# Sixteen gate projections as plain products instead of groups of seven

## The chip, the cores and the metric

The kernel runs on one core of a Trainium2 chip. The metric is the device time of one execution in microseconds; a lower time is better. The core has a matrix engine (TensorE, in the profile PE, with its weight loads as PEld), two elementwise engines (VectorE, DVE, and ScalarE, ACT), GpSimd (POOL) and SyncE (SP), which here only issue transfers for the most part, and 16 DMA engines.

## The reference

One layer of a decoder trunk over 256 positions and 2048 channels. One projection of the normed input h feeds four branches; each is projected to 2048 channels, multiplied by a sigmoid gate that is itself a projection of h, and the four are summed.

```python
h = rmsnorm(x, norm_g)
proj = einsum('bsd,df->bsf', h, w_in)              # 2048 -> 18432
ya = stick_breaking_attention(a_q, a_k, a_v) * silu(a_g)
yb = conformer_conv(b_a, b_b, ...) * silu(b_g)      # 31 taps, LayerNorm over channels
yc = spatial_gating(gelu(c_u), gelu(c_v), ...) * silu(c_g)
yd = dilated_mixture(d_q, d_k, d_v) * silu(d_g)
yproj = einsum('bsnc,ncd->bsnd', stack([ya, yb, yc, yd], 2), w_branch)
gates = sigmoid(einsum('bsd,df->bsf', h, w_gate) + b_gate)   # 2048 -> 4 x 2048
merged = sum(gates * yproj, over n)
out = rmsnorm(x + einsum('bsd,de->bse', merged, w_out), final_g)
```

Everything is float32.

## The kernel before

**Jobs.** The weights lie in HBM as 256 tiles of 128 x 2048 float32, 1 MB each. A *job* is one tile with its matmuls. To keep float32 accuracy, a tile is split into two numbers of a shorter type: ACT rounds it (`hi`, L127), DVE subtracts (`lo`, L134). The moving or stationary side of the product is split in the same way (`xhl` for h, `yh` and `yl` for a branch), and three products stand for one. A projection that leaves channels on the partitions (`proj_t`, `mm_t`, L281 and L284) issues 16 pairs of matmuls of 512 and 256 columns; one that leaves positions there (`mm_n`, L333 to L335) issues 24 matmuls of 512 columns, into two PSUM banks, one for each half of the positions. A gate chunk of 512 channels is four such jobs (`gate_plain`), a branch chunk two (`branch`).

**Order.** The order on PE, ACT, DVE and SP is the order of the program text as `run` (L167) emits it. `prog` is the list of jobs. At step t it issues the loads of jobs up to t + 5, the roundings up to t + 2, the additions up to t + 4 and the subtractions up to t + 2, then the matmuls of job t, its `post`, and what `later` has put down for this step. All four engines work through their queue in that order. POOL, which issues the smaller transfers, is ordered by a planner. Weight tiles have six buffers (`st`), `hi` and `lo` three each; the pool `phase` has two of 128 x 2048, which the branches' `yh` and `yl` share with the masks of the attentions and the constants of the spatial gating.

**Groups.** The gates of the branches b and a, 2 x 2048 channels, are computed in four groups. A group covers two chunks of 512 channels and all 256 positions as a 2 x 2 block product with seven products instead of eight (`group`, L427). Each product has two half jobs of 12 matmuls (`half`, L458). Some use a sum or a difference of weight tiles: `do_load` then loads a second tile, and `do_add` (L122) adds the two on DVE. The matching sums of h are made once by `make_sx` (L382), in four steps, one per job, after the norm of the convolution. The bias enters through one more matmul (L452). Results are combined on DVE (`done`, L441) after copies by ACT (`keep`, L437). The half jobs wait in `queue`; `put` (L160) takes one after every second ordinary job, from the last pair of dilated heads on, and `step(len(queue))` takes the rest ahead of branch a. A half job counts 0.5 in `later`.

**Banks and y.** `n_banks(i)` gives two banks of `ps_n` or `ps_t`; gates always take `n_banks(1)`, branches too, except c. `job_y` (L597) is an empty job ahead of a branch's first one: at `do_add` it loads the branch's y from HBM, and at `do_lo` it splits it into `yh` and `yl`.

**Sequence.** d_v, a_v; b_a and b_b; the dilated heads with the convolution's taps between them on DVE; gates d; b_g; branch d; the stick-breaking heads in pairs (`a_pair`); c_v; branch b; the spatial gating (`c_begin`, `c_norm`, eight `c_unit`); gates c; branch a; branch c; the output projection. The gates' bias of c and d is loaded by `fetch` (tag `ml`, two buffers) and added by DVE (L539); branches use tag `ml` as well, for the running sum that they load from HBM, add to and store (L631, L649, L651).

Of the kernel before, what the change touches and what calls it, by code (L numbers as in the profile page):

```python
# [9 lines left out]
F32 = mybir.dt.float32  # L10
# [15 lines left out]
NEG = -1.0e30  # L26
LOAD_AHEAD = 5
ADD_AHEAD = 4
# [28 lines left out]
def hybrid_block(ctx: ExitStack, tc, w, x, xT, vec, bg, bgb, cst, dmask, sgu_wT, sgu_lg, sgu_lb, sgu_b, final_g, out):  # L57
# [44 lines left out]
    class Job:  # L102
# [3 lines left out]

        def __init__(self, src, mm, plus=None, post=None, keep=None, split=None, prev=None, size=1.0):
            self.src, self.mm, self.plus, self.post, self.keep, self.split = src, mm, plus, post, keep, split
            self.prev, self.size, self.cut = prev, size, False

        def do_load(self):
            src = self.src
            self.st = None if src is None else src() if callable(src) else load(src)
            self.other = load(self.plus) if self.plus is not None else None
            if self.keep is not None:
                self.keep(self.st)

        def do_add(self):
            if self.other is not None:
                if self.prev is not None and not self.prev.cut:  # L120
                    self.prev.do_lo()
                V.tensor_add(self.st[:], self.st[:], self.other[:])  # L122
# [6 lines left out]
        def do_lo(self):  # L129
            if self.split is not None:  # L130
                if not self.cut:
                    self.hl = self.split(self.st)
            elif not self.cut:
                V.tensor_sub(self.hl[1], self.st[:], self.hl[0].bitcast(F32))  # L134
            self.cut = True

    prog, queue, calls = [], [], {}
    now, mains = [0], [0]
# [16 lines left out]
    def step(n=1):  # L155

        for _ in range(min(n, len(queue))):
            prog.append(queue.pop(0))

    def put(job):  # L160

        prog.append(job)
        mains[0] += 1
        if mains[0] % 2 == 0:
            step()

    def run():  # L167
        n = len(prog)
        stages = ((LOAD_AHEAD, "do_load"), (SPLIT_AHEAD, "do_hi"), (ADD_AHEAD, "do_add"), (SPLIT_AHEAD, "do_lo"))
# [207 lines left out]

    sx = {}  # L380

    def make_sx():  # L382

        def pair(name):
            t = st_p.tile([P, 2, KB, P], F32, tag="st", name=name)
            return t[:, 0], t[:, 1]

        def quarter(q, k0, t0):
            V.tensor_add(q, xhl[:, k0:k0 + KB, t0:t0 + P].bitcast(F32), xhl[:, k0:k0 + KB, S + t0:S + t0 + P].bitcast(F32))

        def put(name, src):
            t = s_p.tile([P, 2, KB, P], F32R, tag="s", name=name)
            split(t[:, 0], t[:, 1], src)
            sx[name] = t

        def s1():
            a21, a22 = box["a21"], box["s1"] = pair("a2")
            quarter(a21, 0, P)
            quarter(a22, KB, P)
            V.tensor_sub(a22, a21, a22)  # L400
            put("s1", a22)

        def s2():
            a11, _ = box["a11"], box["a12"] = pair("a1")
            quarter(a11, 0, 0)
            V.tensor_sub(box["s1"], box["s1"], a11)
            put("s2", box["s1"])

        def s3():
            V.tensor_sub(box["a11"], box["a11"], box["a21"])  # L410
            put("s3", box["a11"])

        def n4():
            quarter(box["a12"], KB, 0)
            V.tensor_add(box["a12"], box["a12"], box["s1"])
            put("n4", box["a12"])

        for i, fn in enumerate((s1, s2, s3, n4)):
            later(i + 1, fn)

    def x_part(name):
        if name in ("a11", "a12", "a22"):
            k0, t0 = (0 if name == "a11" else KB), (P if name == "a22" else 0)
            return lambda k, part: xhl[:, k0 + k, part * S + t0:part * S + t0 + P]
        return lambda k, part: sx[name][:, part, k, :]

    def group(expect, sink, bias=None):  # L427


        box, ts, bs = {}, {}, {}  # L430

        def tile_of(c, h, j):
            return expect(c, 2 * h + j)

        def keep(name):
            t = box[name[1]] = so_p.tile([P, 512], F32, tag="so", name=name[1])
            A.activation(t[:], box[name[0]][:], AF.Copy)  # L437

        def done(tb, c, op, a, b, t):
            if op is not None:  # L440
                op(box[t][:], box[a][:], box[b][:])  # L441
            sink(tb, c, box[t], op is not None)

        def half(acc, name, j, src, plus=None, first=False, post=None, keep=None, prev=None):
            def mm(hi, lo):
                lh = x_part(name)
                if first and j == 0:
                    pool, tag = (ps_x, "x") if acc == "X" else (ps_n, "n")
                    ps = box[acc] = pool.tile([P, 512], F32, tag=tag, name=acc)
                    if bias is not None and acc != "Y":  # L450
                        r = bias + (8 if acc == "Z" else 0)
                        T.matmul(ps[:], sel[:, r:r + 1].to_broadcast([P, P]), bgr[:], start=True, stop=False)  # L452
                ps = box[acc]
                fresh = first and j == 0 and (bias is None or acc == "Y")
                for kk in range(4):
                    k, o = 4 * j + kk, kk * 512
                    for i, (part, w_) in enumerate(((0, hi), (0, lo), (1, hi))):
                        T.matmul(ps[:], lh(k, part), w_[:, o:o + 512], start=fresh and kk == i == 0,  # L458
                                 stop=j == 1 and kk == 3 and i == 2, skip_group_check=not first)

            return Job(src, mm, plus=plus, post=post if j else None, keep=keep, prev=prev, size=0.5)

        def held(j):
            return lambda: ts[j]

        V_ = V
        p1 = [half("X", "a11", j, tile_of(0, 0, j), first=True, keep=lambda st, j=j: ts.__setitem__(j, st),
                   post=lambda: keep(("X", "p1"))) for j in range(2)]
        p2 = [half("Y", "a12", j, tile_of(0, 1, j), first=True,
                   post=lambda: done(0, 0, V_.tensor_add, "Y", "p1", "p1")) for j in range(2)]  # L470
        p5 = [half("Z", "s1", j, held(j), plus=tile_of(1, 0, j), first=True, prev=p1[j],
                   post=lambda: keep(("Z", "p5"))) for j in range(2)]
        p6 = [half("X", "s2", j, held(j), plus=tile_of(1, 1, j), prev=p5[j],
                   post=lambda: keep(("X", "u2"))) for j in range(2)]
        p3 = [half("Z", "n4", j, tile_of(1, 1, j),
                   post=lambda: done(0, 1, V_.tensor_sub, "Z", "u2", "u2")) for j in range(2)]
        p7 = [half("X", "s3", j, tile_of(1, 0, j), plus=tile_of(1, 1, j),
                   post=lambda: done(1, 1, V_.tensor_sub, "p5", "X", "p5")) for j in range(2)]
        p4 = [half("X", "a22", j, held(j), plus=tile_of(0, 1, j), prev=p6[j],
                   post=lambda: done(1, 0, None, "X", "X", "X")) for j in range(2)]  # L480
        return p1 + p2 + p5 + p6 + p3 + p7 + p4


# [3 lines left out]

    bgr = cp.tile([P, 512], F32R, name="bgr")
    sel = cp.tile([P, 16], F32R, name="sel")

    def gate_bias_load():
        b0, b1 = box["b0"], box["b1"] = [so_p.tile([P, 512], F32, tag="so", name=f"b{i}") for i in range(2)]
        nc.gpsimd.dma_start(b0[:], bg[0])
        nc.gpsimd.dma_start(b1[:], bg[1])

    def gate_bias():


        b0, b1 = box["b0"], box["b1"]
        V.tensor_add(b0[:], b0[:], b1[:])  # L500
        A.activation(sel[:], cst_sb[:, C_SEL:C_SEL + 16], AF.Copy)
        A.activation(bgr[:], b0[:], AF.Copy)
        V.tensor_sub(bgr[32:64, :], b0[32:64, :], bgr[32:64, :].bitcast(F32))

    def gate_group(b, cc):
        bi = BRANCH[b]

        def sink(tb, c, t, in_sbuf):
            def fn():
                g = t if in_sbuf else so_p.tile([P, 512], F32, tag="so", name="g")  # L510
                A.activation(g[:], t[:], AF.Sigmoid)
                o = (2 * cc + c) * 512
                nc.scalar.dma_start(g_dr[bi, tb, :, o:o + 512], g[:])
                stored.add((b, 2 * cc + c, tb))

            later(1, fn)
# [480 lines left out]
    for i in range(8):  # L997
        c_unit(i)
# [168 lines left out]
```

## Time and profile before

| | us |
|---|---|
| median of three runs | 1589.12 |
| their range | 1582.57 to 1590.14 |
| the profiled execution | 1586.43 |
| its span, first to last instruction | 1583.4 |
| ACT busy (49%) | 776.1 |
| weight loads by SP, 1 MB each | 286 issues, 5.0 to landing (median) |

The mean granted clock of TensorE is 0.976. A matmul's time in the trace is longer than the distance between two starts, because matmuls are pipelined; distances are what counts for throughput. In a row of the trace, the bracket gives the time that the engine was idle just before and the instruction that ended it. In the windows, each engine's busy time in a stretch is followed by its number of instructions.

### The profile page before, as it was taken

To read this page: it belongs to the slowest core of one execution; us is meant where nothing else is said; L and a number is where in the kernel's file an instruction comes from. 1 tells how busy PE (TensorE), PEld (TensorE's weight loads), DVE (VectorE), ACT (ScalarE), POOL (GpSimd) and SP (SyncE) were. 2 spreads that over 40 slices of the span, in tenths; PEclk is the share of its full clock that TensorE was granted. 3 is DMA by queue.
4 is the path that set the end of the run, shared out by engine and by line. 5 is a ranking of instruction groups with operands and counts; after the bars stand their busy time and mean duration, and the time that the engine had idled before them with its cause. 6 is when DMAs were issued, how large, how long until landed. Compare 5 with 4: busy or idle time off the path is not lost.

```text
span 1583.4 us, 18279 instructions
## 1 busy us (share of the span) xinstructions
PE 1487.2 (94%) x7340; PEld 1246.4 (79%) x7340; DVE 1080.6 (68%) x1146; ACT 776.1 (49%) x712; POOL 91.6 (6%) x168
## 2 busy tenths in 40 slices
PE   8999999999998899989999899998799998998997
PEld 6788888888886688777788787877678887876785
DVE  7848888888887776565664665666586765746554
ACT  6444444444444554455446466554266754524442
POOL 0010000000000000001100000011200000021000
PEclk9999999999999899999999999999999999999999
DMA  8675554545452467677864673687875776997551
GB/s 330 214 288 195 185 187 170 193 167 196 162 181 89 169 241 284 246 287 264 283 233 181 251 268 141 234 298 274 314 289 215 267 267 229 365 337 272 187 202 53
DMA packets 62467, 364.60 MB, mean 230 GB/s; under 512 B 8144, under 2 KB 8272, under 8 KB 24880
## 3 DMA queue, kind: packets, MB, share of 16 engines
q1 hardware_dynamic: 43488, 305.29, 52.1%
q0 software_dynamic: 13568, 48.71, 9.2%
q10 hardware_dynamic: 5328, 9.45, 1.6%
q8 instruction: 57, 0.93, 0.2%
q14 instruction: 26, 0.21, 0.0%
HBM read 337.21 MB, written 26.21 MB: 230 GB/s over the span
## 4 chain that ended last, share of the span: by engine, by line
PE 35%; DVE 6%; DMA 6%; ACT 4%; issue 3%; POOL 0%; DVEq 0%; ACTq 0%; POOLq 0%
PE ps L281 6%; DVE lo L134 3%; PE ps L284 3%; PE psy L334 3%; PE X L458 3%; PE psy L333 3%; DMA st<-in_w_dram 3%; PE psy L335 3%; ACT hi L127 2%; PE pso L334 2%; PE pso L335 2%; PE pso L333 2%; PE psg L334 2%; PE psg L333 2%; PE psg L335 2%
## 5 line engine op out<-in xcount | busy, mean ns | idle before, releaser
L134 DVE TENSOR_TENSOR lo<-st,hi 128x2048 fp32r<-128x2048 f32 x272 | 621.2, 2292 | 249.0 <-ACT hi L127 248.9
L281 PE MATMUL ps<-xhl,hi 128*128 128x512 f32 x1920 | 697.5, 406 | 14.9 <-ACT hi L127 5.8
L127 ACT ACTIVATE hi<-st 128x2048 fp32r<-128x2048 f32 x272 | 517.0, 1910 | 249.8 <-PE psy L335 95.3
L284 PE MATMUL ps<-xhl,lo 128*128 128x256 f32 x1920 | 526.9, 285 | 25.9 <-DVE lo L134 25.8
L281 PEld LDWEIGHTS ps<-xhl,hi 128*128 128x128 f32 x1920 | 364.8, 192 | 95.7 <-ACT hi L127 11.4
L284 PEld LDWEIGHTS ps<-xhl,lo 128*128 128x128 f32 x1920 | 369.7, 193 | 41.2 <-DVE lo L134 32.4
L313 ACT ACTIVATE bt<-ps 128x256 f32<-128x256 f32 x120 | 45.8, 382 | 332.1 <-PE ps L281 326.9
L122 DVE TENSOR_TENSOR st<-st 128x2048 f32<-128x2048 f32 x32 | 73.2, 2288 | 76.7 <-DMA st<-in_w_dram 76.7
L333 PE MATMUL psy<-hi,yh 128*128 128x512 f32 x256 | 103.8, 405 | 15.8 <-DVE gl L647 9.3
L689 DVE SCALAR_TENSOR_TENSOR cv<-glu,vec_sb,cv 128x255 f32<-128x255 f32 (+14 forms) x240 | 112.3, 468 | 6.6
L334 PE MATMUL psy<-lo,yh 128*128 128x512 f32 x256 | 103.0, 402 | 5.6 <-DVE lo L134 5.6
L334 PE MATMUL psg<-lo,xhl 128*128 128x512 f32 x256 | 101.1, 395 | 6.1 <-DVE lo L134 6.1
L333 PE MATMUL psg<-hi,xhl 128*128 128x512 f32 x256 | 101.4, 396 | 1.9 <-ACT hi L127 1.9
L335 PE MATMUL psy<-hi,yl 128*128 128x512 f32 x256 | 102.3, 400 | 0.0
L335 PE MATMUL psg<-hi,xhl 128*128 128x512 f32 x256 | 100.9, 394 | 0.0
L314 DVE TENSOR_TENSOR dst<-ps,bt 128x256 f32<-128x256 f32 x120 | 50.6, 421 | 72.9 <-ACT bt L313 72.6
L333 PEld LDWEIGHTS psy<-hi,yh 128*128 128x128 f32 x256 | 49.8, 194 | 30.8 <-ACT hi L127 13.7
L334 PEld LDWEIGHTS psy<-lo,yh 128*128 128x128 f32 x256 | 49.7, 194 | 16.8 <-DVE lo L134 6.8
L334 PEld LDWEIGHTS psg<-lo,xhl 128*128 128x128 f32 x256 | 48.9, 191 | 17.1 <-DVE lo L134 7.0
L333 PEld LDWEIGHTS psg<-hi,xhl 128*128 128x128 f32 x256 | 48.8, 191 | 12.6 <-issue 2.3
L335 PEld LDWEIGHTS psy<-hi,yl 128*128 128x128 f32 x256 | 49.9, 195 | 10.7
L333 PE MATMUL psv<-hi,xuh 128*128 128x512 f32 x128 | 51.6, 403 | 7.0 <-ACT hi L87 7.0
(261 smaller groups left out, 1645.7 us busy)
## 6 DMA issues: line engine op xcount, KB each, us to landing
st<-in_w_dram SPq DMA_DIRECT2D x286, 1024.0 KB, 5.0
gl<-g_dr POOLq DMA_DIRECT2D x32, 256.0 KB, 6.3
m_dr<-gl POOLq DMA_DIRECT2D x24, 256.0 KB, 6.2
ml<-m_dr POOLq DMA_DIRECT2D x24, 256.0 KB, 6.2
g_dr<-g ACTq DMA_DIRECT2D x20, 256.0 KB, 7.0
bgb<-in_bgb_dram POOLq DMA_DIRECT2D x8, 256.0 KB, 7.4
g_dr<-p ACTq DMA_DIRECT2D x8, 256.0 KB, 5.4
xr<-in_x_dram POOLq DMA_DIRECT2D x8, 256.0 KB, 5.0
```

The costliest lines, as they stand in the source:

```text
L122: V.tensor_add(self.st[:], self.st[:], self.other[:])
L127: A.activation(self.hl[0], self.st[:], AF.Copy)
L134: V.tensor_sub(self.hl[1], self.st[:], self.hl[0].bitcast(F32))
L281: T.matmul(ps[:], hi[:, o:o + P], rhs[:, k, :], start=start, stop=stop)
L284: T.matmul(ps[:, 0:S], lo[:, o:o + P], rhs[:, k, 0:S], start=False, stop=False)
L313: A.activation(bt[:], ps[:, S:2 * S], AF.Copy)
L314: V.tensor_add(dst[:, j, :], ps[:, 0:S], bt[:])
L333: T.matmul(ps[tb][:], lh(k0 + kk, 0, tb), hi[:, o:o + 512], start=st, stop=False)
L334: T.matmul(ps[tb][:], lh(k0 + kk, 0, tb), lo[:, o:o + 512], start=False, stop=False)
L335: T.matmul(ps[tb][:], lh(k0 + kk, 1, tb), hi[:, o:o + 512], start=False, stop=sp)
L458: T.matmul(ps[:], lh(k, part), w_[:, o:o + 512], start=fresh and kk == i == 0, stop=j == 1 and kk == 3 and i == 2, skip_group_check=not first)
L689: V.scalar_tensor_tensor(dst, src, wc, dst, op0=ALU.mult, op1=ALU.add)
```

## The change

The groups go, with all that serves them: `make_sx`, `x_part`, `group`, `gate_group`, the bias tiles, `do_add`, the queue of half jobs. All sixteen gate chunks are `gate_plain`, with the bias added by DVE. `put` appends only, so that the order is the written one, and that order is new: gates b stand behind branch d; gates c 0 and c 1, branch b, gates a, branch a, gates c 2 and c 3 follow the spatial gating. Gates and branches take the two pairs of banks in turn, by their chunk. `job_y` is put two jobs ahead of the branch, and loads, rounds and subtracts in the stages of any other job, so that y is split four jobs ahead. Two steps of the convolution's norm are two jobs apart instead of one, and the product with b_g comes two jobs after its hook instead of three.

```diff
+Y_AHEAD = 2
 LOAD_AHEAD = 5
-ADD_AHEAD = 4
+ROUND_AHEAD = 2
...
-            self.other = load(self.plus) if self.plus is not None else None
...
-        def do_add(self):
-            if self.other is not None:
-                if self.prev is not None and not self.prev.cut:
-                    self.prev.do_lo()
-                V.tensor_add(self.st[:], self.st[:], self.other[:])
...
     def put(job):
-
         prog.append(job)
-        mains[0] += 1
-        if mains[0] % 2 == 0:
-            step()
...
-        stages = ((LOAD_AHEAD, "do_load"), (SPLIT_AHEAD, "do_hi"), (ADD_AHEAD, "do_add"), (SPLIT_AHEAD, "do_lo"))
+        stages = ((LOAD_AHEAD, "do_load"), (ROUND_AHEAD, "do_hi"), (SPLIT_AHEAD, "do_lo"))
...
     def gate_plain(b, c):
...
-                    acc["ps"] = n_banks(1, "psg")
+                    acc["ps"] = n_banks(c, "psg")
...
-        def cut(st):
+        def round_y():
             yhl.extend(phase(n, F32R) for n in ("yh", "yl"))
-            split(yhl[0][:], yhl[1][:], box["yf"][:])
-            return ()
-
-        job.do_add, job.split = fetch_y, cut
+            A.activation(yhl[0][:], box["yf"][:], AF.Copy)
+            job.hl = ()
+
+        def rest_y():
+            V.tensor_sub(yhl[1][:], box["yf"][:], yhl[0][:].bitcast(F32))
+
+        job.do_load, job.do_hi, job.do_lo = fetch_y, round_y, rest_y
...
-                    acc[c] = n_banks(c if sink else 1, "psy")
+                    acc[c] = n_banks(c, "psy")
...
-        prog.append(job_y(b, yhl))
+        prog.insert(len(prog) - Y_AHEAD, job_y(b, yhl))
...
-        later(1, lambda: conv_norm_r(csq))
+        later(2, lambda: conv_norm_r(csq))
...
-        later(1, lambda: conv_norm3(red))
+        later(2, lambda: conv_norm3(red))
...
         put_y("b", 0, KB, cv[:])
-        make_sx()
...
-        if h0 == 6:
-            for b in "ba":
-                queue += gate_group(b, 0) + gate_group(b, 1)
...
-            later(3, fn)
+            later(2, fn)
...
     branch("d", first=True)
+
+    for c in range(4):
+        gate_plain("b", c)
...
     v_plain("c_v", AF.Gelu_apprx_tanh)
-    branch("b")
...
     for i in range(8):
         c_unit(i)
+    gate_plain("c", 0)
+    gate_plain("c", 1)
+    branch("b")
     for c in range(4):
-        gate_plain("c", c)
-    step(len(queue))
+        gate_plain("a", c)
     branch("a")
+    gate_plain("c", 2)
+    gate_plain("c", 3)
```

More of the change, by code (lines that the diff above doesn't have):

```diff
@@ L102, in hybrid_block, with __init__ @@
     class Job:
-        def __init__(self, src, mm, plus=None, post=None, keep=None, split=None, prev=None, size=1.0):
-            self.src, self.mm, self.plus, self.post, self.keep, self.split = src, mm, plus, post, keep, split
-            self.prev, self.size, self.cut = prev, size, False
+        def __init__(self, src, mm, post=None, keep=None, split=None, size=1.0):
+            self.src, self.mm, self.post, self.keep, self.split, self.size = src, mm, post, keep, split, size
         def do_load(self):
@@ L130, in do_lo @@
             if self.split is not None:
-                if not self.cut:
-                    self.hl = self.split(self.st)
-            elif not self.cut:
+                self.hl = self.split(self.st)
+            else:
                 V.tensor_sub(self.hl[1], self.st[:], self.hl[0].bitcast(F32))
-            self.cut = True
-    prog, queue, calls = [], [], {}
-    now, mains = [0], [0]
+    prog, calls, now = [], {}, [0]
     def later(n, fn):
@@ L153, in when @@
             later(0.5, lambda: when(ready, fn))
-    def step(n=1):
-        for _ in range(min(n, len(queue))):
-            prog.append(queue.pop(0))
     def put(job):
         prog.append(job)
-        mains[0] += 1
-        if mains[0] % 2 == 0:
-            step()
     def run():
         n = len(prog)
-        stages = ((LOAD_AHEAD, "do_load"), (SPLIT_AHEAD, "do_hi"), (ADD_AHEAD, "do_add"), (SPLIT_AHEAD, "do_lo"))
+        stages = ((LOAD_AHEAD, "do_load"), (ROUND_AHEAD, "do_hi"), (SPLIT_AHEAD, "do_lo"))
         begun = [0] * len(stages)
@@ L374, in first_job @@
         return Job(src, mm, split=cut)
[L380 to L481, printed above, removed]
@@ L486, in hybrid_block @@
     m_dr = dr_p.tile([2, P, D], F32, name="m_dr")
[L488 to L516, printed above, removed]
-        return group(lambda c, q: ("gateN", bi * 4 + 2 * cc + c, q), sink, bias=bi * 2 + cc)
     def gate_plain(b, c):
@@ L671, in hybrid_block @@
           6: lambda: h_split(1), 7: lambda: h_split(2), 8: lambda: h_split(3), 9: h_rstd,
-          10: lambda: d_out(0), 11: lambda: d_out(1), 12: lambda: a_out(0), 13: gate_bias_load,
-          15: lambda: later(1, lambda: (a_out(1), gate_bias()))}
+          10: lambda: d_out(0), 11: lambda: d_out(1), 12: lambda: a_out(0), 15: lambda: later(1, lambda: a_out(1))}
     for i, fn in at.items():
```

## The prediction

> **What bounds the kernel now.** The page first, its busy shares.
>
> ```profile
> span 1583.4 us, 18279 instructions
> PE 1487.2 (94%) x7340; PEld 1246.4 (79%) x7340; DVE 1080.6 (68%) x1146; ACT 776.1 (49%) x712; POOL 91.6 (6%) x168
> ```
>
> PE is the engine that sets the time, so the question is where it loses any. The windows by stage say it: PE busy time is the second number, PEclk the granted clock.
>
> ```profile
> core 0: us, PE busy (x) PEld busy (x) DVE busy (x) ACT busy (x) POOL busy (x), PEclk, DMA share, GB/s
> 120.00:480.00 360.00, 359.91 (x2063) 314.02 (x2062) 301.51 (x512) 163.84 (x178) 3.86 (x6) 1.00 0.51 181
> 480.00:560.00 80.00, 64.54 (x324) 53.91 (x323) 57.13 (x70) 35.90 (x40) 0.54 (x1) 0.89 0.36 133
> 560.00:690.00 130.00, 123.41 (x551) 101.97 (x550) 83.68 (x59) 60.58 (x46) 3.42 (x6) 0.99 0.72 262
> 740.00:800.00 60.00, 55.94 (x231) 45.40 (x231) 35.87 (x24) 25.56 (x17) 7.89 (x15) 0.94 0.75 269
> 800.00:1000.00 200.00, 187.59 (x996) 159.49 (x995) 122.88 (x93) 114.62 (x107) 5.13 (x9) 0.97 0.60 221
> 1060.00:1165.00 105.00, 86.60 (x376) 70.90 (x376) 67.52 (x57) 44.08 (x32) 16.10 (x28) 0.92 0.78 283
> 1290.00:1380.00 90.00, 84.46 (x357) 68.93 (x356) 55.37 (x31) 42.46 (x29) 3.21 (x6) 0.96 0.77 286
> 1380.00:1485.00 105.00, 93.97 (x403) 74.21 (x403) 63.55 (x55) 34.32 (x23) 20.33 (x38) 0.97 0.80 295
> ```
>
> Read the first row against the others. From 120 to 480 only plain projection jobs run, with the convolution and most of the dilated attention beside them on DVE (84% busy), and PE never stops. The products of the groups begin later, by the first start in their row of the tile view:
>
> ```profile
> L458 PE MATMUL X<-hi,xhl x128: 387/389/476, 518.3 to 1378.2; 128*128 128x512 f32 x128
> ```
>
> In the seven rows below the first, PE stands still for 15.5 + 6.6 + 4.1 + 12.4 + 18.4 + 5.5 + 11.0 = **73.5 us**. After a longer stall it also runs at half rate: one minus PEclk times the length gives 8.8 + 1.3 + 3.6 + 6.0 + 8.4 + 3.6 + 3.2 = 35 us. That counts idle time inside a slow stretch twice, as this 5 us window shows, where 2.5 us are charged while PE works 0.84:
>
> ```profile
> 525.00:530.00 5.00, 0.84 (x2) 0.34 (x2) 2.40 (x2) 2.84 (x4) 0.00 (x0) 0.50 0.00 0
> ```
>
> Weighing the slow windows by the work in them I get about 25 us (bounds 15 and 35). So about **98 us** of PE time are lost in these rows.
>
> Who makes PE wait? One such place in the timeline, DVE's rows and then PE's:
>
> ```profile
> 675.43 2.29 DVE L122 TENSOR_TENSOR st<-st 128x2048 f32<-128x2048 f32 x1 [7.53 <-DMA st<-in_w_dram]
> 677.64 2.28 DVE L134 TENSOR_TENSOR lo<-st,hi 128x2048 fp32r<-128x2048 f32 x1
> 679.84 1.28 DVE L539 TENSOR_TENSOR g<-psg,bgb 128x512 f32<-128x512 f32 x2
> ```
>
> ```profile
> 680.67 0.47 PE L281 MATMUL ps<-xhl,hi 128*128 128x512 f32 x1 [4.05 <-DVE g L539]
> ```
>
> The addition of two weight tiles (L122), which only the groups need, stood in DVE's queue for 7.5 us until its second tile had landed. The split and the gate's eviction stood behind it, and PE stood behind them. Over the run L122 has 76.7 us of such waits (its row is below). A product lasts half as long as a job, yet asks for a full split and often for two loads.
>
> **The change part by part.** *More PE work.* A matmul of 512 columns costs this much at full clock:
>
> ```profile
> 1119.15 0.39 PE L334 MATMUL psy<-lo,yh 128*128 128x512 f32 x1
> ...
> 1120.96 0.39 PE L458 MATMUL X<-hi,s 128*128 128x512 f32 x1
> ```
>
> Eight starts in 1.81 us: 0.226 us each. A group is 7 products of 24 matmuls and two for the bias, 170; four groups are 680. The same gates as plain products are 4 x 8 jobs x 24 = 768. **+88 matmuls, +19.9 us**, all on the bounding engine.
>
> *Less work elsewhere.* The rows:
>
> ```profile
> L134 DVE TENSOR_TENSOR lo<-st,hi 128x2048 fp32r<-128x2048 f32 x272 | 621.2, 2292 | 249.0 <-ACT hi L127 248.9
> L127 ACT ACTIVATE hi<-st 128x2048 fp32r<-128x2048 f32 x272 | 517.0, 1910 | 249.8 <-PE psy L335 95.3
> L122 DVE TENSOR_TENSOR st<-st 128x2048 f32<-128x2048 f32 x32 | 73.2, 2288 | 76.7 <-DMA st<-in_w_dram 76.7
> L539 DVE TENSOR_TENSOR g<-psg,bgb 128x512 f32<-128x512 f32 x16 | 10.6, 687 | 1.6 <-PE psg L335 1.6
> ```
>
> 56 half jobs become 32 jobs: 24 splits go (DVE 24 x 2.29 = 55 us, ACT 24 x 1.91 = 46 us), the 32 additions go (73 us), and 32 repeated loads of 1 MB. New are 32 additions of the bias at 0.69 us (22 us); 12 additions of products of about the same length and 12 copies on ACT go. So DVE loses over 110 us and ACT over 45 us. Neither ends last, so by itself none of this is credited. What it buys is that the stalls go, and I price those stage by stage.
>
> *480 to 560.* Two stalls:
>
> ```profile
> 502.15 0.79 PE L281 MATMUL ps<-xhl,hi 128*128 128x512 f32 x1 [5.07 <-DVE dst L314]
> ...
> 527.63 0.80 PE L281 MATMUL ps<-xhl,hi 128*128 128x512 f32 x1 [5.44 <-ACT hi L127]
> ```
>
> The first is the convolution's norm: its reciprocal root, a product of 2.3 us and eight SiLU on ACT stand ahead of a split. That code stays. With two jobs instead of one between its steps, the reduction over channels no longer stands directly ahead of it, and I leave it 4.5 us and 2.9 of slow clock. The second lies in make_sx (four sums of x, each with a split, one per job), which goes. This row falls from 15.5 + 6 to about 7.5.
>
> *560 to 690 and 740 to 800.* The additions go, and the gates alternate between two pairs of banks, so the next chunk needs no eviction. One handover stays behind the gates of d and one behind those of b: the first projection takes the bank of the last chunk's first half and waits for one L539, 0.7 us, with its latency 0.9. Branch d waited for a late y split and for its own eviction (4.1 us in its row); y is now rounded four jobs ahead and the banks alternate: nothing left.
>
> *800 to 1000.* One pair of attention heads puts Abs, Exp and Ln with two table loads ahead of a split; ACT's first row is the end of a projection, DVE's the split that came late, PE's the price.
>
> ```profile
> 854.71 0.38 ACT L313 ACTIVATE bt<-ps 128x256 f32<-128x256 f32 x1 [3.25 <-PE ps L281]
> ```
>
> ```profile
> 863.04 2.29 DVE L134 TENSOR_TENSOR lo<-st,hi 128x2048 fp32r<-128x2048 f32 x1 [7.03 <-ACT hi L127]
> ```
>
> ```profile
> 865.39 0.39 PE L284 MATMUL ps<-xhl,lo 128*128 128x256 f32 x1 [1.54 <-DVE lo L134]
> ```
>
> The chain began at 854.7, and the split was ready at 865.3, 10.6 us later. Two full jobs of 5.6 us (360 us / 2063 x 32 in the clean row) with the score products cover 11.9; a half job in between does not. I leave 1 us a pair, 4 in all (bounds 0 and 12.4).
>
> *1060 to 1165.* Here the groups' additions and second loads met branch b and the gating norm; the last row is the landing time of a branch's load:
>
> ```profile
> 1108.18 0.77 PE L333 MATMUL psy<-hi,yh 128*128 128x512 f32 x1 [5.02 <-DVE gl L647]
> ...
> 1149.43 0.45 PE L284 MATMUL ps<-xhl,lo 128*128 128x256 f32 x1 [4.42 <-DVE lo L134]
> ```
>
> ```profile
> ml<-m_dr POOLq DMA_DIRECT2D x24, 256.0 KB, 6.2
> ```
>
> After the change v is stored just ahead of the norm instead of eight jobs before. Two evictions of 0.7 us, a store and a load of 6.2 us each end some 14 us after v's last product; the norm's place on DVE comes 11.2 us after it. DVE would wait 3 us, with two jobs of split in hand: 1 us for PE (bounds 0 and 5). v keeps one pair of banks: 0.9 us twice.
>
> *1290 to 1485.* Branch c needed its y in the two buffers that branch a still held, and its transposes cost a little:
>
> ```profile
> ACT yh L87 <- PE psy L334: 15.2, 1, 15.2
> ```
>
> ```profile
> 1471.69 0.50 PE L333 MATMUL psy<-hi,yh 128*128 128x512 f32 x1 [1.88 <-DVE ml L1020]
> ```
>
> Eight gate jobs now lie between branch a and branch c, so the wait of 15.2 us goes. The transposes stay: 1.9 us shown, and I allow nearly as much for the other three, 3.3 in all.
>
> *Order and queues.* POOL's place for each load is the planner's. Tag ml has two buffers, for the bias and for a branch's running sum, and a gate's bias is now asked for while branch b or a still runs:
>
> ```profile
> L649 DVE TENSOR_TENSOR gl<-gl,ml 128x512 f32<-128x512 f32 x24 | 16.6, 692 | 1.4 <-DMA ml<-m_dr 0.6
> ```
>
> At best it comes after the sum and costs nothing. At worst it holds one of the two buffers, so in two chunks of two branches the second load begins only after the first addition: 4 x 7 us of DVE waiting, with at most the same on PE. I take 2, because these additions have waited only 0.6 us in all for ml so far. SP issues fewer loads, at 190 GB/s plus 70 for a branch, below the 283 to 295 of the rows above.
>
> **Sum.** Left over: 7.5 + handovers 3.6 (four) + 4 + 1 + 3.3 + 2 = 21 us of 98. Saved 77, paid 19.9: span 1583.4 - 57 = 1526. The profiled execution took 1586.43, 3.0 more than its span, which makes **1529**; the median of the three runs shown, 1589.12, is 2.7 above that execution, inside their spread of 7.6. I forecast 1530.
>
> The clock deserves a look of its own:
>
> ```profile
> 804.79 0.55 PE L284 MATMUL ps<-xhl,lo 128*128 128x256 f32 x1 [1.97 <-DVE lo L134]
> 805.00:810.00 5.00, 5.00 (x21) 4.29 (x22) 4.14 (x2) 0.00 (x0) 0.00 (x0) 0.67 0.97 369
> ```
>
> A stall of 2 us was already followed by half rate, 1.65 us lost. The Trainium skill ("TensorE: Matmul & The Clock Gate", "What's actually happening") says that the clock falls after at least one idle window of about 3.4 us; the row does not agree, and the row decides. By the rule only the stalls above that length (5.07, 5.44, 4.05, 5.02 and 4.42 among the rows shown) would carry clock losses, by my estimate 15 us instead of 25, and the sum would be 1539.
>
> **The rivals.** *A: half of the stalls come back.* The stages keep their own burdens (a norm, a softmax with table loads, 0.75 MB of extra traffic per chunk and pair), and the y splits, the norm with its late v and the ml buffers cost more than I gave them. For it: the 5.07 us stall has nothing to do with the groups. Against it: 120 to 480, with as dense side work, lost nothing. Half of 98 saved: 1586.4 + 19.9 - 49 = 1557; a third saved: 1574.
>
> *B: slower.* The stalls belong to the stages, and the half jobs only happened to be what PE waited at. Then taking them out returns less than the 19.9 us it costs, and from savings below 20 us on the change loses; with none saved 1606. For it: 12.4 us at the attention pairs, where the releaser is L134 behind Exp and Ln. Against it: the 76.7 us that DVE stood before L122 cannot outlive L122. The Trainium skill ("Perfetto Trace Analysis", "Optimization Strategy") says that regimes bound by different engines may gain by being interleaved, which speaks for the old order; the rows so far show the interleaved stretches as the ones that stall, so the trace does not agree.
>
> **How the numbers follow.** Forecast 0.70 (1510 with almost nothing left over, to 1548 with 20 us more than I allowed or the smaller clock term); A 0.22, mostly between 1548 and 1574; B 0.08. The likeliest is 1530. The range 1510 to 1568 leaves out B, the end of A and a little below. What a measurement of this kernel can tell from no change is 0.5%, 8 us: faster takes the forecast and nearly all of A, 0.90; within 0.5% is the end of A and the start of B, 0.03; slower 0.07.
>
> **What would show it.** The profile after should have about 88 more matmuls, no L122, some 24 fewer splits, PE windows as full as 120 to 480 from 560 on, and one stall of 4 to 6 us at the convolution's norm. Wrong would be: repeated PE stalls in the branches with loads of ml or gl as the last releaser (A), waits at the splits in the attention pairs as long as now (B), or DMA shares near 1 while PE waits.

## The result and the profile after

| | before | after |
|---|---|---|
| median of four executions | 1586.69 us | 1509.70 us |
| ratio (95% interval) | | 0.951 [0.9473, 0.9546] |
| profiled execution | 1586.43 us | 1509.23 us |
| its span | 1583.4 us | 1507.3 us |
| mean granted clock | 0.976 | 0.995 |

One of the four executions after was disturbed (3805.53 us); it is left out of the ratio, and the other three lie between 1506.80 and 1510.16.

The forecast was 1530, with a range of 1510 to 1568. The sign came as predicted, and so, in the main, did the mechanism, but the gain is 77 us where the prediction's sum had 57: the time lies 0.3 us below the range. Those 0.3 us are less than the spread of the executions; the 20 us to the forecast are not.

The page of the changed kernel, its busy shares, the chain that ended last, and the lines of the subtraction and of PE's first matmul:

```profile
span 1507.3 us, 18226 instructions
PE 1476.0 (98%) x7428; PEld 1248.4 (83%) x7428; DVE 946.2 (63%) x1080; ACT 704.2 (47%) x657; POOL 94.8 (6%) x174
...
PE 88%; DVE 5%; DMA 3%; ACT 2%; issue 1%; POOL 0%; DVEq 0%; ACTq 0%
...
L125 DVE TENSOR_TENSOR lo<-st,hi 128x2048 fp32r<-128x2048 f32 x248 | 566.9, 2289 | 375.9 <-ACT hi L119 366.0
L261 PE MATMUL ps<-xhl,hi 128*128 128x512 f32 x1920 | 682.4, 401 | 4.7 <-DVE dst L294 4.3
```

PE has the 88 more matmuls (7428 against 7340) and yet is busy for 11.2 us less; its idle time fell from 1583.4 - 1487.2 = 96.2 to 1507.3 - 1476.0 = 31.3. Idle -64.9 and busy -11.2 are the 76.1 by which the span shrank. The subtraction runs 24 times less (248 against 272), as predicted.

The windows of the changed kernel, cut at its own stages (columns as before):

```profile
480.00:540.00 60.00, 55.62 (x304) 48.13 (x304) 39.45 (x57) 28.18 (x34) 0.54 (x1) 0.94 0.49 177
540.00:690.00 150.00, 149.80 (x722) 125.65 (x722) 80.11 (x65) 67.86 (x60) 12.05 (x22) 1.00 0.69 245
690.00:800.00 110.00, 110.00 (x487) 91.09 (x486) 54.07 (x32) 43.53 (x28) 7.03 (x13) 1.00 0.70 240
800.00:1000.00 200.00, 199.52 (x1082) 171.98 (x1081) 100.04 (x86) 109.42 (x107) 9.78 (x16) 1.00 0.54 194
1000.00:1120.00 120.00, 120.00 (x662) 103.80 (x662) 77.03 (x83) 79.29 (x77) 11.95 (x21) 1.00 0.68 243
1120.00:1320.00 200.00, 199.22 (x879) 164.67 (x878) 110.52 (x78) 78.64 (x48) 29.62 (x55) 1.00 0.82 282
1320.00:1410.00 90.00, 86.10 (x380) 69.90 (x379) 56.44 (x44) 35.06 (x26) 10.19 (x19) 0.98 0.76 263
```

From 540 to 1320 PE stands still for 1.5 us in 780, at full clock. Before, these stages held the attention pairs, branch b and the gates, and lost in every row that the prediction shows. What is left behind the start is one stall at the convolution's norm, the transposes of the merged sum in branch c (L862, L866), and two short waits for a split; the waits of PE show them (us in total, times, longest):

```profile
PE psv L313 <- ACT hi L88: 7.6, 2, 6.4
PE ps L261 <- DVE dst L294: 4.3, 1, 4.3
PE psv L314 <- DVE lo L125: 2.7, 4, 1.1
PE psy L313 <- DVE ml L866: 1.9, 1, 1.9
PE pt L862 <- DVE gl L491: 1.3, 2, 0.7
PE psg L314 <- DVE lo L125: 1.2, 2, 0.8
...
PE ps L261 <- DVE g L380: 0.4, 2, 0.2
PE cc L748 <- DVE pr_a L739: 0.3, 1, 0.3
```

The first and the third row belong to the first 80 us of the kernel, as before. Gone is what was the largest row of this view of the kernel before:

```profile
PE ps L284 <- DVE lo L134: 25.8, 14, 5.3
```

### The profile page after: what moved, and what is told of

It is laid out like the page before. It is cut to its first block, busy times and chain, and to the rows that moved or that the text cites. A ratio compares the mean times of both kernels' runs of the same rounds, so it can differ in the third digit from the quotient of the medians.

```text
span 1507.3 us, 18226 instructions
## 1 busy us (share of the span) xinstructions
PE 1476.0 (98%) x7428; PEld 1248.4 (83%) x7428; DVE 946.2 (63%) x1080; ACT 704.2 (47%) x657; POOL 94.8 (6%) x174
## 4 chain that ended last, share of the span: by engine, by line
PE 88%; DVE 5%; DMA 3%; ACT 2%; issue 1%; POOL 0%; DVEq 0%; ACTq 0%
PE ps L261 29%; PE ps L264 14%; PE psg L314 7%; PE psg L315 7%; PE psg L313 7%; PE psy L313 3%; PE psy L315 3%; PE psy L314 3%; DMA ml<-m_dr 2%; PE psv L314 2%; PE psv L315 2%; PE pso L314 2%; PE pso L315 2%; PE pso L313 2%; PE psv L313 2%; DVE lo L125 2%
## 5 line engine op out<-in xcount | busy, mean ns | idle before, releaser
L125 DVE TENSOR_TENSOR lo<-st,hi 128x2048 fp32r<-128x2048 f32 x248 | 566.9, 2289 | 375.9 <-ACT hi L119 366.0
L261 PE MATMUL ps<-xhl,hi 128*128 128x512 f32 x1920 | 682.4, 401 | 4.7 <-DVE dst L294 4.3
L119 ACT ACTIVATE hi<-st 128x2048 fp32r<-128x2048 f32 x248 | 473.5, 1911 | 323.3 <-PE psg L315 181.4
L264 PE MATMUL ps<-xhl,lo 128*128 128x256 f32 x1920 | 519.5, 281 | 0.0
L261 PEld LDWEIGHTS ps<-xhl,hi 128*128 128x128 f32 x1920 | 357.3, 189 | 83.0 <-DVE dst L294 4.6
L264 PEld LDWEIGHTS ps<-xhl,lo 128*128 128x128 f32 x1920 | 363.5, 189 | 9.3
L314 PE MATMUL psg<-lo,xhl 128*128 128x512 f32 x512 | 199.4, 390 | 1.2 <-DVE lo L125 1.2
L313 PE MATMUL psg<-hi,xhl 128*128 128x512 f32 x512 | 199.8, 390 | 0.0
L315 PE MATMUL psg<-hi,xhl 128*128 128x512 f32 x512 | 199.2, 389 | 0.0
L314 PEld LDWEIGHTS psg<-lo,xhl 128*128 128x128 f32 x512 | 96.1, 188 | 21.9 <-DVE lo L125 2.1
L315 PEld LDWEIGHTS psg<-hi,xhl 128*128 128x128 f32 x512 | 96.1, 188 | 20.1
L313 PEld LDWEIGHTS psg<-hi,xhl 128*128 128x128 f32 x512 | 96.1, 188 | 19.6
L314 PE MATMUL psy<-lo,yh 128*128 128x512 f32 x256 | 100.3, 392 | 0.0
L314 PEld LDWEIGHTS psy<-lo,yh 128*128 128x128 f32 x256 | 48.5, 189 | 10.1
```

The source lines that it names most:

```text
L119: A.activation(self.hl[0], self.st[:], AF.Copy)
L261: T.matmul(ps[:], hi[:, o:o + P], rhs[:, k, :], start=start, stop=stop)
L264: T.matmul(ps[:, 0:S], lo[:, o:o + P], rhs[:, k, 0:S], start=False, stop=False)
L313: T.matmul(ps[tb][:], lh(k0 + kk, 0, tb), hi[:, o:o + 512], start=st, stop=False)
L314: T.matmul(ps[tb][:], lh(k0 + kk, 0, tb), lo[:, o:o + 512], start=False, stop=False)
L315: T.matmul(ps[tb][:], lh(k0 + kk, 1, tb), hi[:, o:o + 512], start=False, stop=sp)
```

## The experiments

Two theories, numbered so in the expectations. *Theory 1, the queue:* what PE lost came from waits in DVE's queue (the addition for its second tile, above all), from one pair of banks and from y split late; the change takes these waits away. *Theory 2, the work:* half jobs and additions simply ask more of DVE and ACT than half a job of PE covers, so only less work helps. The runs named b_ and g_ start from the kernel before, those named a_ from the changed one. Ratios are to the kernel before, run beside each on the same chip.

| run | median us | ratio (95%) | span, us | clock |
|---|---|---|---|---|
| b_no_second_load | 1551.32 | 0.9784 [0.9761, 0.9808] | 1552.4 | 0.981 |
| b_no_add | 1546.24 | 0.9749 [0.9726, 0.9771] | 1543.9 | 0.982 |
| b_add3 | 1544.61 | 0.9740 [0.9717, 0.9763] | 1541.1 | 0.983 |
| g_plain_only | 1534.50 | 0.9676 [0.9650, 0.9701] | 1532.2 | 0.991 |
| g_tuned | 1537.20 | 0.9689 [0.9668, 0.9710] | 1537.5 | 0.986 |
| a_banks1 | 1526.76 | 0.9639 [0.9622, 0.9656] | 1523.9 | 0.994 |
| a_make_sx | 1521.01 | 0.9583 [0.9562, 0.9604] | 1520.3 | 0.991 |
| a_branches_adjacent | 1517.51 | 0.9579 [0.9563, 0.9595] | 1516.1 | 0.991 |
| a_conv1 | 1513.37 | 0.9554 [0.9538, 0.9570] | 1512.5 | 0.993 |
| a_y0 | 1511.26 | 0.9543 [0.9527, 0.9560] | 1511.6 | 0.994 |
| a_same | 1510.47 | 0.9517 [0.9497, 0.9537] | 1505.2 | 0.995 |
| a_same2 | 1510.43 | 0.9529 [0.9504, 0.9555] | 1505.3 | 0.997 |
| a_norm_split | 1509.55 | 0.9508 [0.9482, 0.9534] | 1507.8 | 0.995 |
| a_ml3 | 1507.43 | 0.9506 [0.9484, 0.9528] | 1506.2 | 0.995 |
| a_ml3_norm | 1503.51 | 0.9479 [0.9458, 0.9501] | 1503.0 | 0.995 |

### What the additions cost

b_no_second_load: the addition adds the first tile to itself.

```diff
-            self.other = load(self.plus) if self.plus is not None else None
+            self.other = self.st if self.plus is not None else None
...
```

> The kernel before, but the 32 second tiles are not loaded: the addition adds the first tile to itself, so three of seven products in each group and a fourth take other weights. DVE's work and the half jobs stay. Theory 1 (the additions stood in DVE's queue until the second tile had landed): most of the 76.7 us before L122 and most of PE's stalls go, time 1520 to 1545. Theory 2 (a half job asks for a whole split of 2.3 us DVE and 1.9 us ACT in 2.7 us of PE, whatever is loaded): no more than 15 us go, 1570 or above.

b_no_add: neither the second load nor the addition.

```diff
-            self.other = load(self.plus) if self.plus is not None else None
+            self.other = None
...
```

> The kernel before without the second loads and without the additions, so some products take other weights; 56 half jobs stay. Theory 1: within 8 us of the run without second loads. Theory 2: at least 20 us below that run, since 73 us of DVE work leave; what then still stands between it and the changed kernel, less 19.9 us of PE work, is due to half jobs, banks, y and order.

b_add3: everything is computed, but the additions are issued three jobs ahead (and with them the load of a branch's y, which is issued at the same step).

```diff
-ADD_AHEAD = 4
+ADD_AHEAD = 3
```

> The kernel before with the additions issued three jobs ahead instead of four, one job further behind their loads; everything is computed. Theory 1: the wait before L122 falls from 76.7 to below 45 us and the time by 15 to 40 us, 1550 to 1572. Theory 2: within 8 us of before.

The additions in the groups by line of b_no_second_load, then of b_add3; the last field is DVE's idle time ahead of them, 76.7 us in the kernel before:

```profile
L124 DVE TENSOR_TENSOR st<-st 128x2048 f32<-128x2048 f32 x32 | 73.1, 2285 | 23.1 <-DMA st<-in_w_dram 23.1
```

```profile
L122 DVE TENSOR_TENSOR st<-st 128x2048 f32<-128x2048 f32 x32 | 73.1, 2285 | 10.1 <-DMA st<-in_w_dram 10.1
```

The first run fell between the theories' ranges, 35 us below the kernel before: without a second tile the addition still stood 23.1 us in the queue, for the job's own first tile. The second lies 5 us below the first, inside the 8 us of theory 1. The third one settles it, and by more than theory 1 had expected (1550 to 1572). It keeps every load and every addition, and is as fast as the second, which has neither (1544.61 and 1546.24, intervals that overlap). So, once the additions no longer wait long, their 73 us and the 32 MB of second loads cost nothing that these runs can tell; what cost 42 us, more than half of what the change brings, is that an addition issued four jobs ahead came to the head of DVE's queue before its tiles had landed, with the next subtraction behind it. Theory 2 falls for the additions.

### What the groups cost beyond that

g_plain_only: only the groups go; banks, y, order of the branches and the norm stay as before.

```diff
-        make_sx()
...
-        if h0 == 6:
-            for b in "ba":
-                queue += gate_group(b, 0) + gate_group(b, 1)
...
-            later(3, fn)
+            later(2, fn)
...
     branch("d", first=True)
+    for c in range(4):
+        gate_plain("b", c)
...
-    step(len(queue))
+    for c in range(4):
+        gate_plain("a", c)
```

> The groups alone undone: gates b behind branch d and gates a ahead of branch a as plain products, but one pair of banks, y split two jobs ahead, branch b behind c_v, branches a and c next to each other, and the convolution's norm as before (the product with b_g two jobs after its hook, as in the changed kernel). If the groups made the stalls: 1530 to 1545, with the wait of y for branch a's buffers (about 9 us of PE) and the handovers left. If the stages' own burdens made them (rival A or B): 1557 or above.

The waits of PE in this run:

```profile
PE ps L281 <- DVE dst L314: 5.1, 1, 5.1
PE psy L333 <- DVE gl L647: 4.7, 15, 1.4
PE psy L333 <- ACT hi L127: 3.6, 1, 3.6
...
PE psg L333 <- DVE g L539: 2.2, 11, 0.2
PE psy L334 <- DVE lo L134: 1.9, 1, 1.9
```

1534.50, inside the expectation: with 88 more matmuls it is 52 us below the kernel before. The waits for a split are nearly gone, and in their place stand 26 short ones for evictions (L647, L539), from the single pair of banks. The rows of 3.6 and 1.9 us are the wait of y for branch a's buffers.

g_tuned goes the other way: the groups stay, with the additions three jobs ahead, y split early, the norm's steps two jobs apart, the product with b_g two jobs after its hook and the branches in an order near the new one.

```diff
-ADD_AHEAD = 4
+ADD_AHEAD = 3
+Y_AHEAD = 2
...
-        prog.append(job_y(b, yhl))
+        prog.insert(len(prog) - Y_AHEAD, job_y(b, yhl))
...
-        later(1, lambda: conv_norm3(red))
+        later(2, lambda: conv_norm3(red))
...
-    for c in range(4):
-        gate_plain("c", c)
+    gate_plain("c", 0)
+    gate_plain("c", 1)
+    branch("b")
+    gate_plain("c", 2)
     step(len(queue))
     branch("a")
+    gate_plain("c", 3)
```

> The groups kept, with what else was found: additions three jobs ahead, y split early, branch b behind gates c 0 and 1, one gate chunk between branches a and c, the norm's steps two jobs apart; one pair of banks, as the groups need the other. It has 19.9 us of matmuls less than the changed kernel. If the half jobs themselves still crowd DVE and ACT: 1522 to 1536, slower than the changed kernel. If only the waits for second tiles did harm: 1510 or below.

Its largest waits of PE:

```profile
PE ps L285 <- DVE lo L135: 16.0, 13, 2.0
PE X L459 <- DVE p L442: 8.7, 1, 8.7
```

It stays at 0.9689 (1537.20, just above the 1522 to 1536 expected), against 0.9639 for a_banks1 below, which has plain products with the same early y, the same norm, a similar order and also one pair of banks. So even with their worst wait mended, the groups cost some 8 us (0.005 of 1586) more than the 19.9 us of matmuls that they save. What they still pay for are the half job that has to be split in half a job's time (13 waits, none over 2.0 us), the results that must be combined before a bank comes free (one wait of 8.7 us), and make_sx, which alone costs 10.5 us in the run below; no run takes these three apart inside the groups. Here theory 2 has a part. The Trainium skill ("Perfetto Trace Analysis", "Optimization Strategy") says that interleaving may help a kernel whose most-contended engine changes over time. That condition is not met here, for PE is the busiest engine with the half jobs and without, so g_tuned against a_banks1, 0.005 slower, is no test of the sentence.

### Undoing one part of the change

a_banks1, one pair of banks again:

```diff
-                    acc["ps"] = n_banks(c, "psg")
+                    acc["ps"] = n_banks(1, "psg")
...
-                    acc[c] = n_banks(c, "psy")
+                    acc[c] = n_banks(c if sink else 1, "psy")
```

> The changed kernel with one pair of banks for every gate chunk and for the branches b, a and d, as before. In the run with the groups alone undone, a gate chunk lasted 22.25 us where 96 matmuls take 21.75, and a branch chunk 11.35 to 11.93 where 48 take 10.87. By that 15 handovers of gates at 0.5 us and 11 of branches at 0.5 to 1.1 cost 13 to 20 us: 1523 to 1530. If the banks are hidden anyway: within 4 us of 1509.7.

Two neighbouring matmuls of its timeline (start, length, ..., idle time before), the second one the first on a bank that had to be emptied:

```profile
541.87 0.40 PE L315 MATMUL psg<-hi,xhl 128*128 128x512 f32 x1
542.50 0.51 PE L313 MATMUL psg<-hi,xhl 128*128 128x512 f32 x1 [0.23 <-DVE dst L294]
```

1526.76 lies inside the expectation. The span is 16.6 us longer than after the change. The trace shows only 7.5 us more idle time in PE's timeline (28.7 against 21.2); the other 9.1 us are counted as PE busy (1485.1 against 1476.0). The two rows tell where part of them is: the starts are 0.63 us apart instead of 0.227, so the stop costs 0.40, but only 0.23 of it is shown as idle. The rest, 0.17, is the overlap of two matmuls (0.40 long, 0.227 apart) that has to be built up anew; it counts as PE busy. Taken over all stops whose two rows are both single matmuls, start to start less the idle shown and less 0.227 us (0.117 behind 256 columns), this is 7.2 us in 43 stops here, 2.2 in 12 after the change, and 7.9 in 41 before it. That places 5.0 of the 9.1 us; where the other 4 lie, this count does not show. The Trainium skill ("Perfetto Trace Analysis", "Matmuls") says that independent groups of matmuls should rotate through different banks, so that evacuation overlaps with the next group; this run agrees, with some 17 us.

a_make_sx, the four sums of x put back alone:

```diff
         put_y("b", 0, KB, cv[:])
+        make_sx()
```

> The changed kernel with make_sx put back alone, its sums unused: four steps of 3.6 to 5 us on DVE and 1.1 us on ACT, one per job, behind the convolution's norm. If these steps made the second stall before (5.4 and 1.5 us with slow clock behind): 8 to 13 us above the run of the changed kernel. If it was the half jobs that began there: within 3 us of it.

PE's stops in its timeline behind the norm:

```profile
513.63 0.80 PE L261 MATMUL ps<-xhl,hi 128*128 128x512 f32 x1 [4.28 <-DVE dst L294]
523.64 0.49 PE L610 MATMUL s<-dst 128*128 128x128 f32 x2 [1.53 <-DVE dst L294]
529.39 0.45 PE L635 MATMUL pp<-cst_sb,ph_d 128*128 128x128 f32 x1 [4.82 <-DVE ph_d L629]
530.57 0.45 PE L636 MATMUL pp<-cst_sb,ph_d 128*128 128x128 f32 x1 [0.74 <-DVE ph_d L629]
```

10.5 us over a_same, as expected, and at the place expected: the last three stops are new, together 7.1 us, with a slow clock behind them. Not all of it lies there: a short wait for a split behind branch b (L314, 0.8 us after the change) was 2.1 us in this run.

a_branches_adjacent (the last two gates of c ahead of branch a, so that branches a and c share the y buffers again), a_conv1 (the norm's steps one job apart) and a_y0 (no y ahead):

```diff
-        prog.insert(len(prog) - Y_AHEAD, job_y(b, yhl))
+        prog.insert(len(prog) - (0 if sink else Y_AHEAD), job_y(b, yhl))
...
-    branch("a")
     gate_plain("c", 2)
     gate_plain("c", 3)
+    branch("a")
```

> The changed kernel with gates c 2 and c 3 ahead of branch a, so that branch c follows branch a directly and its y has to wait for the two buffers of branch a's y (its split two jobs ahead, since four would never get the buffers). Before, that place cost 3.6 and 2.0 us of idle time and some slow clock: 6 to 10 us more, 1516 to 1520.

```diff
-        later(2, lambda: conv_norm_r(csq))
+        later(1, lambda: conv_norm_r(csq))
...
-        later(2, lambda: conv_norm3(red))
+        later(1, lambda: conv_norm3(red))
```

> The changed kernel with the steps of the convolution's norm one job apart, as before. In the run with the groups alone undone this place cost 1.4 and 5.1 us of idle time against 4.3 in the changed kernel: 2 to 4 us more, 1511 to 1514.

```diff
-Y_AHEAD = 2
+Y_AHEAD = 0
```

> The changed kernel with y split two jobs ahead of its branch instead of four. Before, branch d lost 2.8 us of idle time to the late split, branch b 1.8 us. If that comes back at all four branches, with slow clock behind some: 5 to 15 us more, 1515 to 1525. If the emptier queues of ACT and DVE take the split in two jobs as well: within 4 us of 1509.7.

The first costs about 7 us; its waits of PE show two new rows, at the first matmuls of a branch:

```profile
PE psy L313 <- ACT hi L119: 3.6, 1, 3.6
...
PE psy L314 <- DVE lo L125: 1.9, 1, 1.9
```

The second costs about 3 us and the third 1, by medians against the 1510.4 of the unchanged runs. By the ratios to the kernel before, the three cost 8 to 10, 4 to 6 and 2 to 4 us. Only the interval of the first parts from those of both unchanged runs; a_conv1 overlaps with a_same2, and a_y0 with both, so these two parts stay undecided. a_y0 shows no wait of PE for a late y split at all, which speaks for the second case of its expectation.

### What the changed kernel still loses

a_same and a_same2 are the changed kernel itself, run on the same chip as a_norm_split and as a_ml3.

> The changed kernel itself, beside the others of this call on the same chip: 1505 to 1511. It is what the three below are read against, and what the four runs that undid one part are read against as a ratio to the kernel before.

> The changed kernel again, beside the two below on the same chip: 1505 to 1511.

a_norm_split spreads the norm's product and its eight SiLU over three jobs, so that a split can pass between them:

```diff
-        V.tensor_mul(cv[:], cv[:], bc8(rs[:]))
-        for i in range(8):
-            A.activation(cv[:, i, :], cv[:, i, :], AF.Silu, ...)
-        put_y("b", 0, KB, cv[:])
+        def part(i0, n):
+            V.tensor_mul(cv[:, i0:i0 + n, :], cv[:, i0:i0 + n, :], rs[:].unsqueeze(1).to_broadcast([P, n, S]))
+            for i in range(i0, i0 + n):
+                A.activation(cv[:, i, :], cv[:, i, :], AF.Silu, ...)
+            put_y("b", i0, n, cv[:, i0:i0 + n, :])
+
+        for h in range(3):
+            later(h + 1, lambda h=h: part((0, 3, 6)[h], (3, 3, 2)[h]))
```

> The changed kernel with the last step of the convolution's norm spread: root as now, then product and SiLU for 3, 3 and 2 of the eight channel groups in the next three jobs. If the one stall left in the middle (4.3 us idle, with 3 us of slow clock) is ACT's and DVE's queue behind that step, it goes: 4 to 8 us less than the changed kernel, 1500 to 1506. If not: no change, within 2 us.

A miss: the time is that of a_same. The stall at the norm did go, but PE then met another one, here in its timeline, with the windows around it:

```profile
1191.75 0.50 PE L314 MATMUL psg<-lo,xhl 128*128 128x512 f32 x1 [2.91 <-DVE lo L125]
```

```profile
1190.00:1195.00 5.00, 3.25 (x10) 2.60 (x11) 5.00 (x3) 0.57 (x1) 0.87 (x2) 0.78 0.63 182
1195.00:1200.00 5.00, 5.00 (x21) 4.04 (x20) 1.10 (x1) 1.06 (x1) 0.00 (x0) 0.87 0.94 354
```

The same place in the changed kernel, DVE's timeline:

```profile
1182.59 0.69 DVE L493 TENSOR_TENSOR gl<-gl,ml 128x512 f32<-128x512 f32 x1 [1.75 <-DMA ml<-m_dr]
1183.20 0.69 DVE L491 TENSOR_TENSOR gl<-psy,gl 128x512 f32<-128x512 f32 x1
1189.19 0.69 DVE L493 TENSOR_TENSOR gl<-gl,ml 128x512 f32<-128x512 f32 x1 [5.31 <-DMA ml<-m_dr]
1189.80 6.69 DVE L125 TENSOR_TENSOR lo<-st,hi 128x2048 fp32r<-128x2048 f32 x3
```

DVE stands 5.31 us for a running sum in tag ml, whose load waited for one of two buffers (the runs below test this), and three subtractions stand behind it. In the changed kernel PE's price here is 0.78 us; where PE reaches this place earlier, it is 2.91 us and a slower clock. Hence a third buffer, alone (a_ml3) and with the split norm (a_ml3_norm):

```diff
-    sm2_p = ctx.enter_context(tc.tile_pool(name="ml", bufs=2))
+    sm2_p = ctx.enter_context(tc.tile_pool(name="ml", bufs=3))
```

> The changed kernel with three buffers instead of two for tag ml. In the changed kernel DVE waits 22.6 us for loads of ml, because a gate's bias holds one of the two buffers while branch b or a runs, and a split that stood behind such a wait held PE up for 0.8 us. If that is so: the waits fall below 3 us, the time by 0 to 2 us. If DVE waits for another reason (DMA bandwidth): 22 us of waits as now.

> Three buffers for ml and the norm's last step spread. The spread alone started the gates 4.4 us earlier against the sum ahead of it, but lost 2.9 us of idle time and some slow clock again behind a wait for ml in the branch. If both readings hold: 4 to 7 us below the changed kernel of this call. If the stalls only move: within 2 us of it.

DVE's waits for ml, 22.8 us in a_same2, are out of the list of a_ml3 and 3.2 us in a_ml3_norm, so it was the buffer that the loads waited for; PE's waits for a split there (L314, 1.2 us after the change) are gone in both. Alone, neither edit can be told from the changed kernel beside it (intervals overlap); together they give 1503.51, some 7 us less, as expected, with intervals that just part (0.9501 and 0.9504). It is the fastest version here, 5.2% below the kernel before.

## Why the prediction came out as it did

**Right.** PE stayed the bound. The added matmuls cost what they should: their number is 88, and in the gates of the changed kernel 23 starts take 5.22 us, 0.227 us each:

```profile
584.67 0.39 PE L313 MATMUL psg<-hi,xhl 128*128 128x512 f32 x1
...
589.89 0.39 PE L315 MATMUL psg<-hi,xhl 128*128 128x512 f32 x1
```

L122's wait was the largest single cause (42 us, b_add3). make_sx's stall went, for 10.5 us. The norm's stall stayed, predicted at 4 to 6 us:

```profile
512.41 0.80 PE L261 MATMUL ps<-xhl,hi 128*128 128x512 f32 x1 [4.28 <-DVE dst L294]
```

The transposes were given 3.3 us and took 1.3 + 1.9. The trouble with two ml buffers came as described (22.6 us of DVE waiting in six places), and cost PE 1.2 us of idle time instead of 2.

**Right for another reason, or wrong without weight.** Branches start without a wait for y, as predicted, but the earlier split is not shown to be the reason: in a_y0, without it, PE does not wait for y either. The prediction counted 32 new additions of the bias; 16 are new (L539 ran 16 times before, L380 runs 32 times after). Neither enters the sum. DVE's busy time fell by 134.4 us and ACT's by 71.9.

**Rivals.** A and B both asked for PE stalls that stay in the stages from 540 on; the windows from 540 to 1320 hold 1.5 us. B's ground, that plain jobs would stall at the same places, fell with g_plain_only already: its window 800 to 1000, 12.4 us of idle time before, is as full as that of the changed kernel.

```profile
800.00:1000.00 200.00, 199.53 (x1083) 172.39 (x1082) 104.85 (x89) 112.38 (x107) 7.12 (x12) 1.00 0.55 191
```

**Wrong: the size.** The span was to be 1526 and is 1507.3, 18.7 us less. The sum splits into three terms that were mis-sized:

| term, us | credited | measured |
|---|---|---|
| idle time saved | 73.5 - 18.4 = 55.1 | 64.9 |
| stops whose overlap is built up anew | 0 | 7.9 - 2.2 = 5.7 |
| slow clock saved | 25 - 2.9 = 22.1 | 11.2 + 19.9 - 5.7 = 25.4 |

The largest miss is the step "Left over", 9 of the 9.8 us of the first row: handovers were given 3.6 us and show 0.2 of idle at each of two, the attention pairs 4 and show 0.3, v ahead of the gating norm 1 and shows none, ml 2 and shows 1.2. All four were allowances worked out from the lengths of the tasks ahead, not from a wait in a row of full jobs. At the attention pairs the full jobs alone were enough, as the window of g_plain_only shows. A handover shows 0.2 us of idle even with one pair of banks (a_banks1: 1.8 us in 9 of gates, 3.6 in 15 of branches), so 0.9 was too much for it anywhere. For v and ml no run shows why they came out smaller. The second is a cost that the sum did not have at all, because it sits in PE's busy time: a stop costs on average 0.17 to 0.19 us more than the idle that the trace shows. The clock term is not measured by itself but is the remainder of PE's busy time; weighing the slow windows by the work in them, 25 us, was nearly right, and with the plain sum of 35 the term would have been too large.

**Not settled.** The single undoings add up to some 39 us by medians (17 + 10.5 + 7 + 3 + 1, the last two undecided), and b_add3 alone gives 42. These are not independent parts of 77: the groups' removal takes the additions and make_sx with it, and a stall taken away in one place can come back at the next, as a_norm_split shows.

## What to carry to other kernels

In an engine that works through its queue in order, an operation on a tile should be issued no earlier than the tile is sure to have landed: one constant, 4 to 3, was worth 42 us here with no work changed. Fewer matmuls are a gain only if the other engines can prepare each of them in its own time, which is to be checked per job and not by busy shares (DVE was 68% busy). And independent accumulations should alternate between banks even where a handover shows only 0.2 us of idle, for it costs nearly twice that.

## What the runs showed of the hardware

A stop of PE costs more than its idle: 0.63 us from start to start with 0.23 shown, because the pipelining of 0.40 us matmuls at 0.227 us starts anew. A stall of 2.91 us was followed by a granted clock of 0.78 and 0.87 in two windows of 5 us (a_norm_split), so a slower clock does not need a stall as long as those of 4 to 5 us in the kernel before. Nor does a stall of one length always bring it. The changed kernel stops for 1.88 us at the transposes in branch c, at 1391.8 in the execution profiled after the change and at 1391.4 in a_same, which is the same kernel. The window behind the stop, first of the one and then of the other:

```profile
1395.00:1400.00 5.00, 5.00 (x16) 3.95 (x15) 1.62 (x1) 0.00 (x0) 0.53 (x1) 0.66 0.61 216
```

```profile
1395.00:1400.00 5.00, 5.00 (x24) 4.14 (x23) 1.18 (x1) 0.96 (x1) 0.53 (x1) 1.00 0.66 243
```

The clock was 0.66 in the one and full in the other, 8 matmuls of the window apart: an estimate of 1.7 us (0.34 of 5) by which two executions of one kernel differ. And 32 MB less of loads and 73 us less of additions moved nothing that can be told once the additions were issued later: b_add3, with both, and b_no_add, with neither, are 1.6 us apart.
